# Two matmuls with the same weights made one of 512 columns, and a down unit moved between the products of the up projection

## The chip, the cores and the metric

The kernel runs on one core of a Trainium2 chip. Its engines work side by side, each through its own queue in a fixed order: TensorE (PE in the profile, its weight loads PEld), VectorE (DVE), ScalarE (ACT), GpSimd (POOL) and SyncE (SP), the last two issuing transfers here. The metric is the device time of one execution in microseconds (us), as a median of several runs.

## The reference

One layer of an encoder on 512 positions with 2048 channels, in float32: a normalisation, an input projection, two token mixers (a convolution module and a neighbourhood attention), an output projection, and then the gated MLP that matters here:

```python
xn = rms_norm(x, ffn_norm_g[l])
up = jnp.einsum("bsd,df->bsf", xn, w_up[l])          # 2048 -> 2 * 5632
up = depthwise_conv(up, ffn_dw_w[l], ffn_dw_b[l])    # 3 taps over positions
gate, val = jnp.split(up, 2, axis=-1)
x = x + jnp.einsum("bsf,fd->bsd", jax.nn.silu(gate) * val, w_down[l])
```

A last normalisation follows.

## The kernel before, in words

**Two parts for each number.** To keep float32 accuracy, each operand of a product is held as a high part (rounded to the matmul's format, fp32r) and a low part (the rest). A product is then three matmuls, in mm3 (L116 to L121): high weights by high data (L119), high weights by low data (L120), low weights by high data (L121). Weights come from memory as units of 128x1024 (raw, L103), and parts (L105) splits each: ScalarE copies it to whi (L108), VectorE subtracts to get wlo (L109). There are three buffers each of whi and wlo. weights() makes units two ahead of their use, in the order of the list plan. So a unit's split can only start when the unit three places before it has been used up.

**The up projection** computes its product by a scheme with seven products in place of eight. The 2048 channels are taken as two halves (even and odd blocks of 128) and the positions as two halves of H = 256. For one block f of 128 gate and 128 value columns, factors (L524) makes the seven weight factors out of four loaded units, with four sums on VectorE (L531 to L537; the running sum is ws). The seven data factors are made once, before the up projection, by halves (L486): each is one tile xc of 128x512 whose first 256 columns are the high part and whose last 256 the low part. up(f) (L562) runs the seven products, each of eight steps of 128 channels with three matmuls of 256 columns into the first half of a PSUM bank (pu), and adds them up on the way: two copies on ScalarE (L576, L577) and seven adds of 128x256 on VectorE (L578 to L585). Products one to six use three PSUM banks in turn, so product four takes the bank of product one; product seven has a bank of its own. hidden(f) (L597) then multiplies by the norm's factor (L599, L600, the latter with -1), convolves gate and value (conv3, L588: one scaled copy on ScalarE and two taps on VectorE each), applies silu (L602) and multiplies (L603).

**The down projection** follows in chunks of CH = 4 blocks. in_two (L606) splits the four results of a chunk into hh and hl. The next chunk's blocks carry its 16 output tiles as eight down units: a unit is one weight unit, two output tiles, four steps and three wide matmuls each, so 24 matmuls of 512 columns (pd). Each output tile is copied by ScalarE (pdc, L621) and added to the sum in memory by an accumulating transfer from POOL (L622).

**Order.** The main loop (L625) goes through 11 chunks of 4 blocks, 44 in all. Within a block come seven products, then the convolution, and behind it two down units of the chunk before. The first chunk has none; in the last chunk the first block has none, the next two have two each, and the four others come behind the last block. The last chunk's own down projection stands at the end, in half positions. A scheduler lays out each engine's queue at build time from this program order and from its own estimate of durations; at run time each engine keeps that order. Almost all small tiles share 79 buffers of 2 KB for each partition (t2).

Of the kernel before, what the change touches and what calls it, by code (L numbers as in the profile page):

```python
# [30 lines left out]
KD = D // P  # L31
NC_ = CONV // P
NP_ = HEADS // 2
NF = FF // P
U = 8
# [5 lines left out]
H = S // 2  # L41
CH = 4
NCH = NF // CH
# [11 lines left out]
POFF = {}  # L55
# [8 lines left out]
def layer(ctx: ExitStack, tc: tile.TileContext, xT, w_in, w_out, w_up, w_down, par, tab, out):  # L64
    nc = tc.nc
    consts = ctx.enter_context(tc.tile_pool(name="consts", bufs=1))
# [4 lines left out]
    psm = ctx.enter_context(tc.tile_pool(name="psm", bufs=3, space=bass.MemoryType.PSUM))  # L71
# [10 lines left out]
    def t2(name, dt=F32):  # L82
        return tp.tile([P, S], dt, tag="t2k", name=name)
# [28 lines left out]
    def unit(src, n):  # L112

        return parts(raw_unit(src, n)[0], n)[:2]

    def mm3(ps, w, wk, mh, ml, start, stop):  # L116
        hi, lo = w[:2]
        a = slice(wk * P, (wk + 1) * P)
        nc.tensor.matmul(ps, hi[:, a], mh, start=start, stop=False)  # L119
        nc.tensor.matmul(ps, hi[:, a], ml, start=False, stop=False)  # L120
        return nc.tensor.matmul(ps, lo[:, a], mh, start=False, stop=stop)  # L121
# [83 lines left out]
    for k in range(KD):  # L205
        x1.append(t2("x"))
        last = pin(nc.sync.dma_start(x1[k], xT[k]))
# [223 lines left out]
    p, n = -1, 0  # L431
# [54 lines left out]
    def halves(src, c):  # L486

        t = t2("xc", F32R)
        nc.scalar.activation(t[:, :H], src, AF.Copy)
        nc.vector.tensor_sub(t[:, H:], src, t[:, :H].bitcast(F32))  # L490
        comb[c].append((t[:, :H], t[:, H:]))

    def after(d, ps):

# [23 lines left out]

    rstd2 = []

    def stats2():
        rstd2.append((yield from rsqrt_steps(acc2, D, "rstd2")))

    def factors(f):  # L524

        def make(c):
            if c == 0:
                a[:] = [raw_unit(w_up[f, q], U * P)[0] for q in range(4)] + [t4([P, U * P], "ws")]
            a11, a21, a22, a12, s_ = a
            if c == 1:  # L530
                add(s_, a21, a22)  # L531
            elif c == 2:
                add(s_, s_, a11)
            elif c == 4:
                add(a21, a21, a11)
            elif c == 5:
                add(s_, s_, a12)  # L537
            return parts((a11, s_, s_, a12, a21, s_, a22)[c], U * P)[:2]

        a = []  # L540
        return [lambda c=c: make(c) for c in range(7)]

    add = nc.vector.tensor_add

    def down_units(c, i):
# [12 lines left out]

    out_half(mb, after)
    steps.append(stats2())  # L560

    def up(f):  # L562

        def product(c):
            w = weights()
            ps = (psa.tile([P, S], F32, tag="po", name="pu") if c == 6 else
                  psm.tile([P, S], F32, tag="mm", name="pu"))[:, :H]
            for k in range(U):
                m = mm3(ps, w, k, *comb[c][k], k == 0, k == U - 1)
            tick(m)  # L570
            return ps

        uu, vv = t2("u"), t2("v")
        u, t, u2 = uu[:, :H], uu[:, H:], vv[:, :H]
        g, v = t2("g"), t2("vl")
        nc.scalar.activation(u, product(0), AF.Copy)  # L576
# [8 lines left out]
        add(v[:, :H], u2, product(6))  # L585
        return g, v

    def conv3(a, n):  # L588
        y = t2("uy")
        o = POFF["fww"] + 3 * n  # L590
        nc.scalar.activation(y, a, AF.Identity, scale=prm[:, o + 1:o + 2], bias=pc("fwb", n))
        nc.vector.scalar_tensor_tensor(y[:, 1:], a[:, :S - 1], prm[:, o:o + 1], y[:, 1:], op0=ALU.mult, op1=ALU.add)
        nc.vector.scalar_tensor_tensor(y[:, :S - 1], a[:, 1:], prm[:, o + 2:o + 3], y[:, :S - 1],
                                       op0=ALU.mult, op1=ALU.add)
        return y

    def hidden(f):  # L597
        g, v = up(f)
        nc.vector.tensor_mul(g, g, rstd2[0])  # L599
        nc.vector.scalar_tensor_tensor(v, v, -1.0, rstd2[0], op0=ALU.mult, op1=ALU.mult)  # L600
        g, v = conv3(g, f), conv3(v, NF + f)
        nc.scalar.activation(g, g, AF.Silu)  # L602
        nc.vector.tensor_mul(g, g, v)  # L603
        return g

    def in_two(g):  # L606
        h, l = t2("hh", F32R), t2("hl", F32R)
        nc.scalar.activation(h, g, AF.Copy)
        nc.vector.tensor_sub(l, g, h.bitcast(F32))
        return h, l  # L610

    def down(hs, ds):

        for d0 in ds:
            w = weights()
            for d in range(d0, d0 + U // CH):
                ps = psa.tile([P, S], F32, tag="tr", name="pd", bufs=2)
                for k in range(CH):
                    mm3(ps, w, (d - d0) * CH + k, *hs[k], k == 0, k == CH - 1)
                t = t2("pdc")  # L620
                nc.scalar.activation(t, ps, AF.Copy)  # L621
# [12 lines left out]
    n = CH  # L634
    x2 = []
# [95 lines left out]
```

## Time and profile before

| what | us |
|---|---|
| median of 3 runs | 2103.06 |
| lowest and highest | 2101.43, 2103.21 |
| the profiled execution | 2101.72 |
| its span, first to last instruction | 2099.9 |
| mean granted TensorE clock | 0.996 of full speed |

How to read the profile: a group row names source line, engine, operation, and output from inputs by tile names, then the shape; after the bar stand the group's busy time with the mean duration of one, and then the idle time of the engine just before such instructions, with what ended it. In the timeline a row starts with the start time and the duration, in us from the start of the span; "[1.90 <-PE pd]" means that the engine was idle for 1.90 us before and that this ended it. Matmuls, and most operations of VectorE and ScalarE, overlap with the one behind them, so a cost is read from start to start, not from the duration.

Where the time lies, by TensorE's starts: 8.5 to 502 us the input projection with the mixers beside it, to 699 the output projection, 699 to 2034 the up and down projections, to 2084 the last chunk's down projection.

### The profile page before, as it was taken

How to read it: one execution, taken by the hardware profiler on the slowest of the kernel's cores; microseconds unless marked ns; L12 is line 12 of the kernel's file. 1: busy time of each engine (PE TensorE's matmuls, PEld its weight loads, DVE VectorE, ACT ScalarE, POOL GpSimd, SP SyncE). 2: the span in 40 equal slices, each digit the busy share in tenths (PEclk: the TensorE clock that was granted, in tenths of full speed). 3: DMA queues.
4: the chain of work that ended last, by engine and by line, in shares of the span. 5: the costliest groups of instructions: out<-in, count | busy, mean ns of one | idle time of the engine just before them, and what ended most of it. 6: DMA issues, size and time to landing. Idle time of an engine off the chain costs nothing.

```text
span 2099.9 us, 32453 instructions
## 1 busy us (share of the span) xinstructions
PE 2061.7 (98%) x13024; PEld 1851.1 (88%) x13024; DVE 1585.8 (76%) x2180; ACT 985.3 (47%) x1428; POOL 140.0 (7%) x166
## 2 busy tenths in 40 slices
PE   8999999999999999999999999999999999999997
PEld 6888888877778899999999999999999999999987
DVE  7985796686568898777777778777777777878756
ACT  6234424447436544444444444454454444545452
POOL 0000000000000000110110110110111011010110
PEclk9999999999999999999999999999999999999998
DMA  6333223335324244555555565665565555554672
GB/s 237 101 111 110 81 81 110 101 101 200 116 96 140 71 121 124 138 130 143 130 139 143 122 146 135 132 140 136 137 140 127 144 131 138 144 121 123 147 193 81
DMA packets 95911, 270.90 MB, mean 129 GB/s; under 512 B 10640, under 2 KB 14736, under 8 KB 95760
## 3 DMA queue, kind: packets, MB, share of 16 engines
q1 hardware_dynamic: 72720, 226.88, 33.7%
q0 software_dynamic: 23040, 41.95, 14.7%
q8 instruction: 102, 1.67, 0.3%
q14 instruction: 49, 0.40, 0.1%
HBM read 218.46 MB, written 50.33 MB: 128 GB/s over the span
## 4 chain that ended last, share of the span: by engine, by line
PE 94%; DVE 4%; DMA 1%; ACT 1%; issue 0%; SPq 0%; DVEq 0%; ACTq 0%
PE pu L121 13%; PE pu L119 13%; PE pu L120 13%; PE pd L119 8%; PE pd L120 8%; PE pd L121 8%; PE pj L119 7%; PE pj L121 7%; PE pj L120 7%; PE po L119 2%; PE po L120 2%; PE po L121 2%; DVE wlo L109 1%; PE sc L365 1%; PE po L408 1%; PE trp L395 1%
## 5 line engine op out<-in xcount | busy, mean ns | idle before, releaser
L121 PE MATMUL pu<-xc,wlo 128*128 128x256 f32 x2464 | 697.8, 283 | 2.1 <-DVE wlo L109 2.1
L108 ACT ACTIVATE whi<-raw 128x1024 fp32r<-128x1024 f32 x368 | 389.4, 1059 | 660.0 <-PE pu L120 299.3
L119 PE MATMUL pu<-xc,whi 128*128 128x256 f32 x2464 | 698.3, 283 | 0.8 <-ACT whi L108 0.7
L120 PE MATMUL pu<-xc,whi 128*128 128x256 f32 x2464 | 698.0, 283 | 0.0
L109 DVE TENSOR_TENSOR wlo<-raw,whi 128x1024 fp32r<-128x1024 f32 x368 | 449.1, 1222 | 171.6 <-ACT whi L108 143.9
L121 PEld LDWEIGHTS pu<-xc,wlo 128*128 128x128 f32 x2464 | 473.3, 192 | 3.2 <-DVE wlo L109 3.2
L119 PEld LDWEIGHTS pu<-xc,whi 128*128 128x128 f32 x2464 | 473.5, 192 | 2.9 <-ACT whi L108 1.2
L120 PEld LDWEIGHTS pu<-xc,whi 128*128 128x128 f32 x2464 | 473.6, 192 | 1.9 <-issue 0.2
L109 DVE TENSOR_TENSOR wlo<-ws,whi 128x1024 fp32r<-128x1024 f32 x132 | 161.5, 1223 | 160.2 <-ACT whi L108 159.7
L622 POOL DMA_DIRECT2D x2d<-pdc x160 | 139.3, 873 | 1896.0 <-ACT pdc L621 1893.4
L119 PE MATMUL pj<-xh,whi 128*128 128x512 f32 x640 | 254.1, 398 | 8.5 <-ACT whi L108 8.5
L121 PE MATMUL pj<-xh,wlo 128*128 128x512 f32 x640 | 250.3, 391 | 1.7 <-DVE wlo L109 1.7
L119 PE MATMUL pd<-hh,whi 128*128 128x512 f32 x640 | 249.6, 390 | 1.9 <-ACT pdc L621 1.9
L120 PE MATMUL pj<-xl,whi 128*128 128x512 f32 x640 | 250.3, 391 | 0.0
L108 ACT ACTIVATE whi<-ws 128x1024 fp32r<-128x1024 f32 x132 | 139.9, 1060 | 233.7 <-PE pd L120 142.4
L120 PE MATMUL pd<-hl,whi 128*128 128x512 f32 x640 | 249.5, 390 | 0.0
L121 PE MATMUL pd<-hh,wlo 128*128 128x512 f32 x640 | 249.0, 389 | 0.0
L279 DVE SCALAR_TENSOR_TENSOR y<-ch,prm,y 128x504 f32<-128x504 f32 (+14 forms) x240 | 170.2, 741 | 3.2
L119 PEld LDWEIGHTS pj<-xh,whi 128*128 128x128 f32 x640 | 120.7, 189 | 37.0 <-ACT whi L108 10.5
L121 PEld LDWEIGHTS pj<-xh,wlo 128*128 128x128 f32 x640 | 120.5, 188 | 29.1 <-DVE wlo L109 3.6
L119 PEld LDWEIGHTS pd<-hh,whi 128*128 128x128 f32 x640 | 120.3, 188 | 26.3 <-ACT pdc L621 2.3
L121 PEld LDWEIGHTS pd<-hh,wlo 128*128 128x128 f32 x640 | 120.1, 188 | 25.3
(141 smaller groups left out, 2403.4 us busy)
## 6 DMA issues: line engine op xcount, KB each, us to landing
raw<-in_w_up SPq DMA_DIRECT2D x176, 512.0 KB, 4.1
raw<-in_w_down SPq DMA_DIRECT2D x88, 512.0 KB, 3.7
raw<-in_w_in SPq DMA_DIRECT2D x80, 512.0 KB, 3.6
x2d<-pdc POOLq DMA_DIRECT2D x160, 256.0 KB, 4.2
raw<-in_w_out SPq DMA_DIRECT2D x32, 512.0 KB, 3.5
x<-in_xT SPq DMA_DIRECT2D x32, 256.0 KB, 6.0
tab<-in_tab SPq DMA_DIRECT2D x32, 256.0 KB, 4.0
x2d<-x SPq DMA_DIRECT2D x16, 256.0 KB, 2.0
```

What stands on the lines that cost most here:

```text
L108: i = nc.scalar.activation(hi[:, :n], raw[:, :n], AF.Copy)
L109: j = nc.vector.tensor_sub(lo[:, :n], raw[:, :n], hi[:, :n].bitcast(F32))
L119: nc.tensor.matmul(ps, hi[:, a], mh, start=start, stop=False)
L120: nc.tensor.matmul(ps, hi[:, a], ml, start=False, stop=False)
L121: return nc.tensor.matmul(ps, lo[:, a], mh, start=False, stop=stop)
L279: nc.vector.scalar_tensor_tensor(y[:, a:b], h[:, a + j - PAD:b + j - PAD], prm[:, o + j:o + j + 1], y[:, a:b], op0=ALU.mult, op1=ALU.add)
L365: m = nc.tensor.matmul(both[:, j, i, :], q[hp, b * P:(b + 1) * P], grid(k, KC0[b], KW)[hp], start=True, stop=True)
L395: m = nc.tensor.transpose(ps[:, 2 * i + ch, :], s[:, i, ch * P:(ch + 1) * P], ident)
L408: m = nc.tensor.matmul(grid(po, b * BLK, BLK)[hp], vt[b // 2][:, 2 * (b % 2) + ch, hp], pts[j][:, 2 * i + ch, :], start=(ch == 0), stop=(c ...
L622: nc.gpsimd.dma_start(xd[d], t, accum_op=ALU.add)
```

## The change

In each of the eight steps of a product of the up projection, the two matmuls with whi (by the high and by the low data) become one of 512 columns over the whole tile xc, so the low data's product comes out in the second half of the PSUM bank; the matmul with wlo adds to that second half. A product therefore leaves a main half and a leftover half that must be added: ScalarE copies the leftover half to a small tile (pl), and VectorE adds. In place of seven adds of 128x256 there are ten of 128x256 and two of 128x512: one makes both value sums by reading its input twice, one adds the two gate leftovers. The minus sign of L600 moves into a copy of the value taps (fwn), made once. The down units are no longer two behind the block: one stands behind the fourth product and one behind the seventh; both are issued inside up, through the callback between. In the last block of the last chunk none runs inside, and in_two stands ahead of the four left over.

```diff
-        comb[c].append((t[:, :H], t[:, H:]))
+        comb[c].append(t)
...
+    fwn = consts.tile([P, 3 * NF], F32, name="fwn")
+    nc.vector.tensor_scalar(fwn, prm[:, POFF["fww"] + 3 * NF:POFF["fww"] + 6 * NF], -1.0, None, op0=ALU.mult)
...
-    def down_units(c, i):
+    def down_units(c, i, at):
-        at = [0, 4, 8, 12, 16] if c < NCH - 1 else [0, 0, 4, 8, 16]
-        return range(at[i], at[i + 1], U // CH) if c else ()
+        n = U // CH
+        if not c:
+            return ()
+        if c < NCH - 1:
+            return {3: (4 * i,), 6: (4 * i + n,)}.get(at, ())
+        return {(1, 3): (0,), (1, 6): (2,), (2, 3): (4,), (2, 6): (6,), (3, 6): range(8, KD, n)}.get((i, at), ())
...
-            plan.extend(factors(c * CH + i))
-            for d0 in down_units(c, i):
-                plan.append(lambda c=c, d0=d0: unit(down_weights((c - 1) * CH, d0), U * P))
+            for at, make in enumerate(factors(c * CH + i)):
+                plan.append(make)
+                for d0 in down_units(c, i, at):
+                    plan.append(lambda c=c, d0=d0: unit(down_weights((c - 1) * CH, d0), U * P))
...
-    def up(f):
+    def up(f, between):
         def product(c):
             w = weights()
             ps = (psa.tile([P, S], F32, tag="po", name="pu") if c == 6 else
-                  psm.tile([P, S], F32, tag="mm", name="pu"))[:, :H]
+                  psm.tile([P, S], F32, tag="mm", name="pu"))
             for k in range(U):
-                m = mm3(ps, w, k, *comb[c][k], k == 0, k == U - 1)
-            tick(m)
-            return ps
+                hi, lo = (w[i][:, k * P:(k + 1) * P] for i in range(2))
+                m = comb[c][k]
+                wide = lambda: nc.tensor.matmul(ps, hi, m, start=k == 0, stop=k == U - 1)
+                low = lambda: nc.tensor.matmul(ps[:, H:], lo, m[:, :H], start=False, stop=False)
+                if k < U - 1:
+                    wide()
+                    i = low()
+                else:
+                    low()
+                    i = wide()
+            tick(i)
+            between(c)
+            return ps[:, :H], ps[:, H:]
+        def low_part(ps):
+            t = t2("pl")[:, :H]
+            nc.scalar.activation(t, ps, AF.Copy)
+            return t
...
-        nc.scalar.activation(u, product(0), AF.Copy)
-        nc.scalar.activation(t, product(1), AF.Copy)
-        add(u2, u, product(2))
+        m, l = product(0)
+        add(u, m, low_part(l))
+        m, l = product(1)
+        add(t, m, low_part(l))
+        m, l = product(2)
+        l = low_part(l)
+        add(u2, u, m)
+        add(u2, u2, l)
         add(t, t, u2)
-        add(g[:, :H], u, product(3))
-        ps = product(4)
-        add(u2, u2, ps)
-        add(v[:, H:], t, ps)
-        add(g[:, H:], t, product(5))
-        add(v[:, :H], u2, product(6))
+        low = t2("pl")
+        m, l = product(3)
+        nc.scalar.activation(low[:, :H], l, AF.Copy)
+        add(g[:, :H], u, m)
+        m, l = product(4)
+        add(u, m, low_part(l))
+        add(v.rearrange("p (i t) -> p i t", i=2), uu, u.unsqueeze(1).broadcast_to([P, 2, H]))
+        m, l = product(5)
+        nc.scalar.activation(low[:, H:], l, AF.Copy)
+        add(g[:, H:], t, m)
+        add(g, g, low)
+        m, l = product(6)
+        l = low_part(l)
+        add(v[:, :H], v[:, :H], m)
+        add(v[:, :H], v[:, :H], l)
         return g, v
...
-        nc.vector.scalar_tensor_tensor(v, v, -1.0, rstd2[0], op0=ALU.mult, op1=ALU.mult)
+        nc.vector.tensor_mul(v, v, rstd2[0])
...
-            hs.append(hidden(c * CH + i))
-            if c == NCH - 1 and i == CH - 1:
-                hs = [in_two(h) for h in hs]
-            down(pend, down_units(c, i))
-        pend = hs if c == NCH - 1 else [in_two(h) for h in hs]
+            last = c == NCH - 1 and i == CH - 1
+            hs.append(hidden(c * CH + i, lambda at: None if last else down(pend, down_units(c, i, at))))
+        hs = [in_two(h) for h in hs]
+        if last:
+            down(pend, down_units(c, i, 6))
+        pend = hs
```

More of the change, by code (lines that the diff above doesn't have):

```diff
@@ L566, in product @@
             ps = (psa.tile([P, S], F32, tag="po", name="pu") if c == 6 else
-                  psm.tile([P, S], F32, tag="mm", name="pu"))[:, :H]
+                  psm.tile([P, S], F32, tag="mm", name="pu"))
             for k in range(U):
-                m = mm3(ps, w, k, *comb[c][k], k == 0, k == U - 1)
-            tick(m)
-            return ps
[L573 to L576, printed above, removed]
@@ new lines, in product @@
+                low = lambda: nc.tensor.matmul(ps[:, H:], lo, m[:, :H], start=False, stop=False)
[12 more added lines that the diff above has]
+            return t
+        u = t2("u")[:, :H]
@@ new lines, in up @@
+        uu = t2("uu").rearrange("p (i t) -> p i t", i=2)
+        u2, t = uu[:, 0], uu[:, 1]
+        g = t2("g")
+        v = t2("vl")
+        m, l = product(0)
[6 more added lines that the diff above has]
+        add(u2, u2, l)
+        add(t, t, u2)
+        low = t2("pl")
+        m, l = product(3)
+        nc.scalar.activation(low[:, :H], l, AF.Copy)
+        add(g[:, :H], u, m)
@@ L590, in conv3, with hidden @@
         o = POFF["fww"] + 3 * n
-        nc.scalar.activation(y, a, AF.Identity, scale=prm[:, o + 1:o + 2], bias=pc("fwb", n))
-        nc.vector.scalar_tensor_tensor(y[:, 1:], a[:, :S - 1], prm[:, o:o + 1], y[:, 1:], op0=ALU.mult, op1=ALU.add)
-        nc.vector.scalar_tensor_tensor(y[:, :S - 1], a[:, 1:], prm[:, o + 2:o + 3], y[:, :S - 1],
+        w, o = (prm, o) if n < NF else (fwn, o - POFF["fww"] - 3 * NF)
+        nc.scalar.activation(y, a, AF.Identity, scale=w[:, o + 1:o + 2], bias=pc("fwb", n))
+        nc.vector.scalar_tensor_tensor(y[:, 1:], a[:, :S - 1], w[:, o:o + 1], y[:, 1:], op0=ALU.mult, op1=ALU.add)
+        nc.vector.scalar_tensor_tensor(y[:, :S - 1], a[:, 1:], w[:, o + 2:o + 3], y[:, :S - 1],
                                        op0=ALU.mult, op1=ALU.add)
         return y
-    def hidden(f):
-        g, v = up(f)
+    def hidden(f, between):
+        g, v = up(f, between)
         nc.vector.tensor_mul(g, g, rstd2[0])
-        nc.vector.scalar_tensor_tensor(v, v, -1.0, rstd2[0], op0=ALU.mult, op1=ALU.mult)
+        nc.vector.tensor_mul(v, v, rstd2[0])
         g, v = conv3(g, f), conv3(v, NF + f)
```

## The prediction

> **What bounds the kernel now.** I read the page from the top: span and busy time, then the chain of work that ended last, then the groups of instructions.
>
> ```profile
> span 2099.9 us, 32453 instructions
> PE 2061.7 (98%) x13024; PEld 1851.1 (88%) x13024; DVE 1585.8 (76%) x2180; ACT 985.3 (47%) x1428; POOL 140.0 (7%) x166
> ...
> PE 94%; DVE 4%; DMA 1%; ACT 1%; issue 0%; SPq 0%; DVEq 0%; ACTq 0%
> PE pu L121 13%; PE pu L119 13%; PE pu L120 13%; PE pd L119 8%; PE pd L120 8%; PE pd L121 8%; PE pj L119 7%; PE pj L121 7%; PE pj L120 7%; PE po L119 2%; PE po L120 2%; PE po L121 2%; DVE wlo L109 1%; PE sc L365 1%; PE po L408 1%; PE trp L395 1%
> ...
> L121 PE MATMUL pu<-xc,wlo 128*128 128x256 f32 x2464 | 697.8, 283 | 2.1 <-DVE wlo L109 2.1
> ```
>
> TensorE is 94% of the chain, the up projection's three matmul lines alone 39%. The group row says the same from the other side: before 2464 matmuls on L121 TensorE was idle for 2.1 us in all. So today what counts is the spacing of the matmuls, not a wait. Their 283 ns is no spacing, because they overlap; that is read from start to start, in the timeline of TensorE across one pair of down units:
>
> ```profile
> 1299.76 0.28 PE L121 MATMUL pu<-xc,wlo 128*128 128x256 f32 x1
> ...
> 1306.96 0.28 PE L121 MATMUL pu<-xc,wlo 128*128 128x256 f32 x1
> 1307.08 0.40 PE L119 MATMUL pd<-hh,whi 128*128 128x512 f32 x1
> 1307.32 0.40 PE L120 MATMUL pd<-hl,whi 128*128 128x512 f32 x1
> ...
> 1317.76 0.39 PE L121 MATMUL pd<-hh,wlo 128*128 128x512 f32 x1
> 1317.99 0.28 PE L119 MATMUL pu<-xc,whi 128*128 128x256 f32 x1
> 1318.10 0.28 PE L120 MATMUL pu<-xc,whi 128*128 128x256 f32 x1
> ```
>
> From 1299.76 to 1306.96 lie 60 narrow (256-column) starts, 0.120 us each; from 1307.32 to 1317.76 lie 46 wide (512-column) ones, 0.227 us each. Two narrow ones cost 0.240, one wide 0.227: about 13 ns per matmul do not depend on its width. That is what the merge can save.
>
> The second view is the windows, for how full VectorE is (the columns are length, then PE, PEld, DVE, ACT, POOL busy, clock, DMA share, GB/s):
>
> ```profile
> 752.00:772.00 20.00, 19.73 (x165) 19.53 (x164) 18.97 (x25) 9.23 (x12) 0.00 (x0) 1.00 0.37 106
> 1300.00:1600.00 300.00, 300.00 (x2074) 281.06 (x2073) 224.03 (x270) 143.56 (x182) 34.49 (x40) 1.00 0.59 137
> ```
>
> In the first chunk, where blocks have no down units, VectorE is busy 95%: there it sets the pace already. Later it is at 75% and TensorE at 100%. ScalarE is at half in both. I call one call of hidden a block; there are 44, four to a chunk.
>
> **The change, part by part. 1. Matmuls removed.** Each of 44 x 7 x 8 = 2464 steps has three narrow matmuls (0.360 us) now and one wide plus one narrow afterwards. No row shows them alternating. By the two spacings the pair is 0.227 + 0.120 = 0.347. At the change of width the rows above show 0.24 for the first wide after a narrow and 0.11 for the first narrow after a wide: 0.350. I take 0.348, between these, so 12 ns saved per step: **-29.6 us** (ends -32.0 and -24.6). A product goes from 2.88 to 2.784 us, a regular block from 31.06 to 30.4.
>
> **2. Work added.** Per block ScalarE gets five more copies of 128x256 out of PSUM; at half busy, and with its time spent in waits for TensorE, it hides them. VectorE's adds go from seven of 128x256 to ten, plus two of 128x512. What that costs is again read from start to start:
>
> ```profile
> 747.37 0.42 DVE L585 TENSOR_TENSOR vl<-v,pu 128x256 f32<-128x256 f32 x1
> ...
> 766.23 1.22 DVE L109 TENSOR_TENSOR wlo<-ws,whi 128x1024 fp32r<-128x1024 f32 x1
> 767.37 0.75 DVE L592 SCALAR_TENSOR_TENSOR uy<-g,prm,uy 128x511 f32<-128x511 f32 x1
> 768.04 0.42 DVE L585 TENSOR_TENSOR vl<-v,pu 128x256 f32<-128x256 f32 x1
> 768.38 0.75 DVE L593 SCALAR_TENSOR_TENSOR uy<-g,prm,uy 128x511 f32<-128x511 f32 x1
> 769.05 0.68 DVE L600 SCALAR_TENSOR_TENSOR vl<-vl,rstd 128x512 f32<-128x512 f32 x1
> 769.65 1.22 DVE L533 TENSOR_TENSOR ws<-ws,raw 128x1024 f32<-128x1024 f32 x1
> 770.78 0.74 DVE L592 SCALAR_TENSOR_TENSOR uy<-vl,prm,uy 128x511 f32<-128x511 f32 x1
> ...
> 788.73 0.42 DVE L585 TENSOR_TENSOR vl<-v,pu 128x256 f32<-128x256 f32 x1
> ...
> 810.33 0.42 DVE L585 TENSOR_TENSOR vl<-v,pu 128x256 f32<-128x256 f32 x1
> ```
>
> A weight split takes 1.14, a convolution tap 0.67, a 128x256 add 0.34, a 128x512 one 0.60, a weight sum 1.13. So the block's VectorE work grows by 3 x 0.34 + 2 x 0.60 = 2.2 us. L585 is the last read of a block, so its rows also give the period: 20.67 and 20.69 for blocks 2 and 3 against 168 x 0.120 = 20.16 of matmuls.
>
> In the first chunk nothing covers the 2.2 us. By these intervals a block without down units has 7 x 1.14 + 4 x 1.13 + 7 x 0.34 + 4 x 0.67 + 3 x 0.60 = 19.4 us now (1.3 of 20.7 idle) and 21.6 afterwards. In the changed order VectorE's read of the sixth product still waits for TensorE, which I put at 0.5 us: 22.1 instead of 20.7. Against the 20.0 that part 1 credits that is 2.1 each for blocks 1 to 3: **+6.3 us**. Block 4 adds the chunk's four hl and meets the first down unit; from L585 of block 3 to the end of block 4's down units it is 21.6 + 10.9 now. Afterwards I count 28.4 to the last product, as product four waits for a bank read that stands behind the hl, and 5.4 for the second down unit: 33.8, against 31.8 credited, **+2.0 us**.
>
> **3. Regular blocks** (29, with two down units each and no chunk boundary). Take the start of a block's first product as zero. Today's rows at the end of a down unit, which ends at 1317.99:
>
> ```profile
> 1317.96 1.06 ACT L108 ACTIVATE whi<-ws 128x1024 fp32r<-128x1024 f32 x1 [1.90 <-PE pd L120]
> 1318.93 0.58 ACT L621 ACTIVATE pdc<-pd 128x512 f32<-128x512 f32 x1
> 1319.06 1.23 DVE L109 TENSOR_TENSOR wlo<-ws,whi 128x1024 fp32r<-128x1024 f32 x1 [2.95 <-ACT whi L108]
> ```
>
> The third product's weights take the down unit's buffer, so VectorE starts its split at 1.07. In the changed order follow: an add (2.21), a tap that waits for ScalarE, then add, tap, multiply, the split for product four, a tap, and at 6.6 the read that frees the first product's PSUM, done at 7.05. Product four, which takes that bank, starts at 8.35: 1.3 us to spare. The split for the down unit ends at 9.8 and is needed at 11.6. VectorE's busy 75% of 31.06 are 23.2 us; with 2.2 more, 25.4 fit into 30.4, and the moved down unit spreads them. **0 us**, and the price if this cover goes is in rival C.
>
> The wait of that tap: ScalarE does the down unit's copy, the sixth product's leftover copy and the convolution's scale first:
>
> ```profile
> 790.45 0.82 ACT L591 ACTIVATE uy<-vl,prm 128x512 f32<-128x512 f32 x1
> 791.17 0.61 ACT L608 ACTIVATE hh<-uy 128x512 fp32r<-128x512 f32 x1
> ...
> 796.09 0.36 ACT L576 ACTIVATE u<-pu 128x256 f32<-128x256 f32 x1
> ```
>
> ScalarE's rows overlap by 0.1 (790.45 + 0.82 against 791.17), so 0.94 + 0.48 + 0.27 + 0.82 = 2.51, and the tap starts at 2.56.
>
> **4. Chunk boundaries.** Before, the first down unit of a chunk stood behind all seven products, some 20 us after in_two began. Now it stands behind the third or fourth, and in the built order of the changed kernel it comes after product three, while VectorE has the four hl subtractions ahead of that unit's weight split. From 2.56: tap 0.67, add 0.34, tap 0.67, multiply 0.60, split 1.14, tap 0.67, hl 0.60, tap 0.67, hl 0.60, multiply 0.60, hl 0.60 makes 9.72; the split ends 1.22 later at 10.94. TensorE arrives at 3 x 2.784 = 8.35, can do four wide matmuls with the high part, and needs the low part at 9.26; with the weight load it goes on at about 11.1: a stall of 1.8 us. Product four behind it waits for the bank read at 11.9, which the next five matmuls cover. Eight boundaries (blocks 8 to 36): **+14.4 us** (ends 0 and 8 x 3 = 24). At block 40 there is no down unit to put first, so product four waits for that bank, from 8.35 to 11.95: **+3.6 us**. Behind block 43 the 21.7 us of down units cover in_two, as now.
>
> **5. The rest at nothing.** The negated taps are made once, 0.2 us beside the first loads; tensor_mul for L600 has the same size. SP's loads of the down weights are asked for two units ahead as before, and by the changed order their buffers come free 10 us or more before the use. POOL has four accumulating transfers per block in two pairs instead of one group, at 7% busy. The new small tiles reuse buffers that such a transfer reads, but by the changed order those lie half a block back, against 4 us of a transfer.
>
> **Sum:** -29.6 + 6.3 + 2.0 + 14.4 + 3.6 = -3.3 us. The profiled execution took 2101.72 us, 1.8 over its span; it comes to 2098.4. The median of the runs shown, 2103.06, is 1.3 above it: **2099.8 us**.
>
> **Rivals.** **B: no stall at boundaries**, because VectorE gets ahead (a shorter wait for the tap, hl earlier). For it: VectorE idles 2.95 us just before zero in the row at 1319.06. Against it: that idle time is a wait for the buffer, which stays. Without the 14.4: 2103.06 - 17.7 = 2085.4.
>
> **C, slower: VectorE also late in regular blocks.** Its place is the read that frees the first product's bank before product four; it decides from a delay of 1.3 us. With 1.7 us of delay, 29 blocks lose 0.4 and eight boundaries 1.7: 25.2 us more, 2125. For it: twelve instructions behind each other with durations from another stage, and new reads of PSUM. Against it: none of them waits long by my count.
>
> **D: the fixed 13 ns is not saved**, because each change of width costs what the first wide one showed (0.24 instead of 0.227) and the narrow one gives nothing back. Then the stalls stand alone: 2103.06 + 26.3 = 2129. Against it is the 0.11 at 1318.10. [...]
>
> That the change does not do what it says is out: in its built order each product has eight wide and eight narrow matmuls.
>
> **How the numbers follow.** Chances: forecast 0.45 (own range 2094 to 2108: both ends of part 1, and half a us at each boundary), B 0.22, C 0.20, D 0.13. The range goes from 2082 (B with 0.347) to 2130 (D); outside lie about a fifth of B, a third of C and part of D, some 0.15. About 0.2%, 4.2 us, is what a measurement of this kernel can tell from no change: faster is below 2098.9, slower above 2107.3. Faster: B and two fifths of the forecast, 0.41; slower: C, D and a sliver, 0.35; within: 0.24.
>
> **What would show it.** Right: pu steps at 0.348 in the timeline; regular blocks of 30.4 from last read to last read; first-chunk blocks of 22; TensorE waiting for wlo about 1.8 us eight times, and about 3.6 once at block 40 for a read of PSUM. Wrong: steps at 0.36 (D), regular blocks over 30.6 with waits for VectorE (C), or boundaries as long as their neighbours (B).

## The result, and the profile after

The changed kernel is slower: 2115.64 us against 2102.62 for the kernel before, medians of four runs each, a ratio of 1.0062 (95% interval 1.0045 to 1.008). The forecast was 2099.8.

The page of the changed kernel's profiled execution (2115.82 us), and the two groups of the up projection's matmuls:

```profile
span 2114.0 us, 27919 instructions
PE 2054.8 (97%) x10560; PEld 1723.3 (82%) x10560; DVE 1664.5 (79%) x2401; ACT 1037.7 (49%) x1648; POOL 140.1 (7%) x166
...
L580 PE MATMUL pu<-xc,whi 128*128 128x512 f32 x2464 | 865.4, 399 | 8.6 <-DVE u L604 5.8
L581 PE MATMUL pu<-xc,wlo 128*128 128x256 f32 x2464 | 644.0, 282 | 2.4 <-DVE wlo L109 2.4
```

The merge did what it says: 2464 wide and 2464 narrow matmuls stand where 7392 narrow ones were. Yet TensorE is still busy 97%, and the idle time in front of a few matmuls is new. The waits of TensorE (total, times, longest, in us) name them:

```profile
PE pd L121 <- DVE wlo L109: 11.6, 8, 1.4
...
PE pu L580 <- DVE u L604: 5.8, 2, 3.4
...
PE pd L119 <- ACT pdc L664: 3.6, 1, 3.6
```

Eight waits of a down unit for wlo are the eight chunk boundaries; the 3.4 for a read of PSUM (L604) is block 40; the wait for pdc is in the last block, and was 1.9 before. Two rows of VectorE's timeline lie a block apart; here are the last reads (L627) of blocks 18, 19, 20 and 21:

```profile
1265.93 0.42 DVE L627 TENSOR_TENSOR vl<-vl,pl 128x256 f32<-128x256 f32 x1
...
1296.56 0.42 DVE L627 TENSOR_TENSOR vl<-vl,pl 128x256 f32<-128x256 f32 x1
...
1328.96 0.42 DVE L627 TENSOR_TENSOR vl<-vl,pl 128x256 f32<-128x256 f32 x1
...
1359.60 0.42 DVE L627 TENSOR_TENSOR vl<-vl,pl 128x256 f32<-128x256 f32 x1
```

A regular block takes 30.63 us, where 30.4 was forecast and 31.06 stood before. The block behind a boundary (20 is the first of a chunk) takes 32.40, 1.77 more than its neighbours. VectorE's queue at that place shows why:

```profile
1299.96 0.69 DVE L652 TENSOR_TENSOR hl<-uy,hh 128x512 fp32r<-128x512 f32 x1
...
1301.22 0.69 DVE L652 TENSOR_TENSOR hl<-uy,hh 128x512 fp32r<-128x512 f32 x1
...
1302.42 0.68 DVE L652 TENSOR_TENSOR hl<-uy,hh 128x512 fp32r<-128x512 f32 x1
1303.03 1.22 DVE L109 TENSOR_TENSOR wlo<-raw,whi 128x1024 fp32r<-128x1024 f32 x1
1304.16 0.68 DVE L652 TENSOR_TENSOR hl<-uy,hh 128x512 fp32r<-128x512 f32 x1
```

Three of the four hl stand ahead of the split (L109) of the down unit's weights, the fourth behind it, and VectorE has no gap. TensorE's own timeline shows both, the spacing and the stall:

```profile
1299.29 0.40 PE L580 MATMUL pu<-xc,whi 128*128 128x512 f32 x1
1299.52 0.28 PE L581 MATMUL pu<-xc,wlo 128*128 128x256 f32 x1
...
1301.06 0.40 PE L580 MATMUL pu<-xc,whi 128*128 128x512 f32 x1
...
1302.46 0.40 PE L120 MATMUL pd<-hl,whi 128*128 128x512 f32 x1
1304.30 0.51 PE L121 MATMUL pd<-hh,wlo 128*128 128x512 f32 x1 [1.45 <-DVE wlo L109]
```

From 1299.29 to 1301.06 lie five steps of a wide and a narrow matmul, 0.354 us each. Over all 1036 pairs from 1240 to 1900 us the wide one takes 0.2352 from start to start and the narrow one 0.1173: 0.3525, not 0.348.

The third cause is in no list of waits. The windows show it. Columns are length, busy time of PE, PEld, DVE, ACT and POOL, then the granted clock. First around the gap at 591 us, where TensorE waits 3.6 us for oa in the output projection, which the change doesn't touch; then around block 40's stall:

```profile
590.87:594.29 3.42, 0.63 (x3) 0.19 (x1) 3.39 (x6) 1.67 (x2) 0.00 (x0) 1.00 0.42 156
594.29:597.70 3.41, 2.62 (x6) 2.15 (x7) 3.38 (x7) 0.00 (x0) 0.00 (x0) 0.50 0.49 154
597.70:601.11 3.41, 3.41 (x9) 2.64 (x8) 0.36 (x1) 0.00 (x0) 0.00 (x0) 0.50 0.00 0
...
1922.07:1925.48 3.41, 1.35 (x8) 0.92 (x6) 3.41 (x6) 2.47 (x6) 0.00 (x0) 1.00 0.00 0
1925.48:1928.90 3.42, 2.08 (x7) 1.81 (x8) 3.39 (x8) 0.40 (x2) 0.00 (x0) 0.50 0.49 153
1928.90:1932.31 3.41, 3.41 (x12) 2.93 (x12) 1.59 (x2) 0.66 (x1) 0.00 (x0) 0.50 0.68 185
```

Behind the slices of 3.41 us in which TensorE was busy for only 0.63 and 1.35 us, the next two ran at half the clock, 0.50. The kernel before has the same gap at 591, but its profiled execution shared it out over two slices, busy 1.68 and 1.56 us each, and the clock stayed up:

```profile
590.03:593.45 3.42, 1.68 (x8) 1.06 (x6) 3.40 (x5) 1.67 (x2) 0.00 (x0) 1.00 0.29 93
593.45:596.86 3.41, 1.56 (x7) 1.33 (x8) 3.41 (x6) 0.00 (x0) 0.00 (x0) 1.00 0.66 215
```

In the changed kernel's profiled execution four places have such slices that the kernel before's has not: 594 (6.83 us), 806 (3.41), 1925 (6.83) and 2031 us (3.41).

Where the time went, in the two profiled executions, by the starts of each block's first matmul on TensorE. The last column is the sum of the prediction's own terms for that stretch:

| stretch | before, us | after, us | difference | forecast |
|---|---|---|---|---|
| up to the first product | 698.78 | 701.36 | +2.6 | 0 |
| blocks 0 to 3 | 89.75 | 91.29 | +1.5 | +3.6 |
| block 4 | 32.51 | 35.84 | +3.3 | +1.3 |
| blocks 5 to 39, eight boundaries among them | 1087.10 | 1086.32 | -0.8 | -9.1 |
| block 40 | 20.15 | 25.85 | +5.7 | +2.9 |
| blocks 41 to 43, to the last matmul of the up projection | 82.16 | 80.76 | -1.4 | -2.0 |
| behind it | 89.51 | 92.60 | +3.1 | 0 |
| sum | 2099.9 | 2114.0 | +14.0 | -3.3 |

### The profile page after: what moved, and what is told of

Its sections match the earlier page's. It is cut to its first block, busy times and chain, and to the rows that moved or that the text cites. A ratio compares the mean times of both kernels' runs of the same rounds, so it can differ in the third digit from the quotient of the medians.

```text
span 2114.0 us, 27919 instructions
## 1 busy us (share of the span) xinstructions
PE 2054.8 (97%) x10560; PEld 1723.3 (82%) x10560; DVE 1664.5 (79%) x2401; ACT 1037.7 (49%) x1648; POOL 140.1 (7%) x166
## 4 chain that ended last, share of the span: by engine, by line
issue 50%; PE 36%; POOL 6%; DVE 4%; DMA 2%; ACT 1%; SPq 0%; POOLq 0%; DVEq 0%; ACTq 0%
PE pj L119 7%; PE pj L121 6%; PE pj L120 6%; POOL x2d L665 6%; PE pu L580 2%; PE po L119 2%; PE po L120 2%; PE po L121 2%; PE pu L581 1%; PE pd L119 1%; PE pd L121 1%; PE pd L120 1%; DVE wlo L109 1%; PE sc L365 1%; PE po L408 1%
## 5 line engine op out<-in xcount | busy, mean ns | idle before, releaser
L580 PE MATMUL pu<-xc,whi 128*128 128x512 f32 x2464 | 865.4, 399 | 8.6 <-DVE u L604 5.8
L581 PE MATMUL pu<-xc,wlo 128*128 128x256 f32 x2464 | 644.0, 282 | 2.4 <-DVE wlo L109 2.4
L109 DVE TENSOR_TENSOR wlo<-raw,whi 128x1024 fp32r<-128x1024 f32 x368 | 448.9, 1221 | 142.7 <-ACT whi L108 113.5
L580 PEld LDWEIGHTS pu<-xc,whi 128*128 128x128 f32 x2464 | 450.9, 189 | 99.6 <-ACT whi L108 4.3
L581 PEld LDWEIGHTS pu<-xc,wlo 128*128 128x128 f32 x2464 | 467.2, 190 | 32.5 <-DVE wlo L109 5.0
L109 DVE TENSOR_TENSOR wlo<-ws,whi 128x1024 fp32r<-128x1024 f32 x132 | 161.5, 1223 | 127.9 <-ACT whi L108 127.9
L120 PEld LDWEIGHTS pd<-hl,whi 128*128 128x128 f32 x640 | 120.6, 188 | 25.4
L120 PEld LDWEIGHTS pj<-xl,whi 128*128 128x128 f32 x640 | 120.8, 189 | 24.6 <-issue 0.7
```

What stands on the lines that cost most here:

```text
L109: j = nc.vector.tensor_sub(lo[:, :n], raw[:, :n], hi[:, :n].bitcast(F32))
L580: wide = lambda: nc.tensor.matmul(ps, hi, m, start=k == 0, stop=k == U - 1)
L581: low = lambda: nc.tensor.matmul(ps[:, H:], lo, m[:, :H], start=False, stop=False)
```

## The experiments

Theory after this reading: a step saves 7.5 ns instead of 12; the moved units add the forecast boundary stalls; and idle stretches cost more than their length, by the clock behind them. Rivals: VectorE is late in every block; the boundary stall comes from the plan of the weights; the half speed belongs to something else.

| kernel | median, us | ratio to the kernel before (95% interval) |
|---|---|---|
| the changed kernel | 2115.64 | 1.0062 (1.0045 to 1.008) |
| e1, merge alone | 2099.90 | 0.9984 (0.9974 to 0.9993) |
| e2, placement alone | 2110.84 | 1.0035 (1.0022 to 1.0048) |
| e3, grouped | 2103.43 | 0.9999 (0.999 to 1.0008) |
| e4, halves spread | 2091.77 | 0.9947 (0.993 to 0.9963) |
| e5, gap filled | 2113.79 | 1.0049 (1.0034 to 1.0064) |
| e6, before, shifted | 2104.08 | 1.0005 (0.9996 to 1.0014) |
| e7, spread and grouped | 2083.93 | 0.9907 (0.989 to 0.9923) |
| e8, combined | 2079.90 | 0.9890 (0.9875 to 0.9904) |
| e10, before, gap filled | 2101.72 | 0.9992 (0.9983 to 1.0001) |

e9 (2109.29 us) and e11 (2107.05 us) are single executions, read from their traces. The kernel before, run beside each group, had medians of 2102.62 to 2103.38.

**e1, the merge alone.** In the changed kernel the plan and the loop of the kernel before:

```diff
-            hs.append(hidden(c * CH + i, lambda at: None if last else down(pend, down_units(c, i, at))))
+            hs.append(hidden(c * CH + i))
+            if c == NCH - 1 and i == CH - 1:
+                hs = [in_two(h) for h in hs]
+            down(pend, down_units(c, i))
```

> The merge alone: the changed kernel with the down units behind the block again, where the kernel before has them. Theory (the changed kernel's trace: a step of a wide and a low matmul takes 0.353 us, not the 0.348 that was forecast; the placed units bring eight boundary stalls of 1.8 us; idle stretches of over 2 us inside one 3.41 us slice of a fixed grid halve the granted clock in the next slices): the boundary stalls and most of the 3.8 us at block 40 go, with them the half-speed slices at 806 and 1925 us (1.7 and 3.4 us), regular blocks stay at 30.63 us: 2092 to 2098 us. Rival (the units have to stand inside the block because VectorE is late in every block with the merged matmul): about 1 us of wait in each of 40 blocks, 2130 us or more.

2099.90 us, 15.7 under the changed kernel and 2 over the theory's stretch. Regular blocks stay at 30.63, the boundary blocks fall to 30.94, block 40 to 20.0: most of the stall belongs to the placement (0.31 us at each boundary stays). VectorE isn't late in every block, so that rival is out. What missed: those 0.31 us, 2.5 at eight boundaries, and block 4, where TensorE waits 3.6 us for a read of PSUM (2.3 in the changed kernel) and a half-speed slice follows, as no unit stands in front.

**e2, the placement alone.** The kernel before, with its narrow matmuls, and the changed kernel's plan, callback and loop:

```diff
             tick(m)
+            between(c)
             return ps
...
-            hs.append(hidden(c * CH + i))
+            hs.append(hidden(c * CH + i, lambda at: None if last else down(pend, down_units(c, i, at))))
```

> The placement alone: the kernel before with its three narrow matmuls, the down units behind the fourth and the seventh product as in the changed kernel. Theory (the four hl of a chunk stand on VectorE ahead of the wlo that the first unit needs, whatever the matmuls are; VectorE has about 1.4 us less to do in a block here): a stall of 0.5 to 1.8 us at each of eight boundaries, 2106 to 2117 us, blocks otherwise at 31.06 us. Rival (placement is harmless, the stall is made by the merge's additional adds): 2102 to 2104 us, and no wait of a down unit for wlo.

2110.84 us: the placement by itself costs 7.5 us. The boundary block takes 31.73 against 31.08, a stall of 0.65. But the wait that shows isn't the one the theory named. The waits of TensorE in this kernel:

```profile
PE pu L119 <- ACT u L582: 4.2, 9, 1.3
```

Nine times (eight boundaries and block 40) it waits for ScalarE's copy of a product. In ScalarE's queue that copy (L582) stands behind the chunk's last hh and a weight copy, and the last hh waits for VectorE's last multiply (L609) among the hl:

```profile
1297.47 0.63 ACT L614 ACTIVATE hh<-uy 128x512 fp32r<-128x512 f32 x1 [0.45 <-DVE uy L609]
1298.17 1.06 ACT L108 ACTIVATE whi<-raw 128x1024 fp32r<-128x1024 f32 x1
1299.13 0.36 ACT L582 ACTIVATE u<-pu 128x256 f32<-128x256 f32 x1
...
1299.55 0.39 PE L119 MATMUL pu<-xc,whi 128*128 128x256 f32 x1 [0.37 <-ACT u L582]
```

The same bunch of work, another end of it. One by one, the edits make -3.5 and +7.5, together +4.0; both at once make +13.0. In the profiled executions 5.9 us of what they make beyond their sum lie in blocks 5 to 39 and 4.3 in block 40; other stretches give a part back. At a boundary it is VectorE's queue: from the split of the third product's weights to that of the down unit's it is 7.38 us long in e2 and 8.61 in the changed kernel (1294.42 to 1303.03), where the last product's two adds and a multiply stand in between.

**e3, grouped.** Seven wide matmuls, the eight low ones, the last wide one:

```diff
-                if k < U - 1:
-                    wide()
-                    i = low()
-                else:
-                    low()
-                    i = wide()
+            for k in range(U - 1):
+                wide(k)
+            for k in range(U):
+                nc.tensor.matmul(ps[:, H:], w[1][:, k * P:(k + 1) * P], comb[c][k][:, :H], start=False, stop=False)
+            i = wide(U - 1)
```

> The changed kernel with the order inside a product changed: seven wide matmuls, then the eight low ones, then the last wide one, so that wide follows wide and low follows low. Theory (the missing 5 to 6 ns of a step come from the alternation of 512 and 256 columns): the step falls from 0.353 to 0.347 us, 56 steps in each of 40 blocks, about 13 us less: 2100 to 2104 us, regular blocks at 30.3 us. Rival (a wide matmul of the up projection takes 0.233 us whatever stands ahead of it): no change, 2114 to 2117 us.

2103.43 us, in the theory's stretch, but not for the theory's reason alone: regular blocks fall to 30.43, a step to 0.3491 and not to 0.347. That is 0.20 us in 40 blocks, 8 us; the rest came from blocks 0 to 4 and 40 and from the stretch up to the first product, where this execution also had fewer half-speed slices (mean clock 0.994 against 0.992). TensorE's timeline, where eight equal matmuls are one row:

```profile
1398.19 2.00 PE L578 MATMUL pu<-xc,whi 128*128 128x512 f32 x8
1400.03 1.11 PE L583 MATMUL pu<-xc,wlo 128*128 128x256 f32 x8
1400.99 2.00 PE L578 MATMUL pu<-xc,whi 128*128 128x512 f32 x8
```

Eight wide ones take 1.84 us, 0.230 each, not 0.227; eight narrow ones 0.96, 0.120. By position, the first five wide ones behind narrow ones take 233, 236, 228, 232 and 231 ns, and from the sixth on it is 226.7. The kernel before has the same five numbers where a down unit follows a product. So in these two traces the first five wide matmuls behind narrow ones took 2 to 9 ns more than the later ones; the first two narrow ones behind a wide run gave 8 ns back (113 and 119 instead of 120).

**e9, in twos.** The same, in short runs:

```diff
+            for k in range(0, U - 2, 2):
+                wide(k)
+                wide(k + 1)
+                low(k)
+                low(k + 1)
+            wide(U - 2)
+            low(U - 2)
+            low(U - 1)
+            i = wide(U - 1)
```

> The changed kernel with wide and low matmuls in twos: runs of three, two, two and one wide per product with two low ones between. Theory (the traces of the kernel before and of e3 show that the first five wide ones behind narrow ones take 233, 236, 228, 232 and 231 ns and only then 226.7): short runs get almost nothing, 697 + 2 x 469 + 234 for the wide and about 944 for the low ones, 2.813 us for a product and 30.57 us for a regular block. Rival (each change of width has a fixed price, half as many changes give half of what no change would): 30.40 us or less, under the 30.43 of e3.

Regular blocks take 30.56 us, forecast 30.57, not 30.40: short runs gain 0.07 us where the grouping of e3 gained 0.20. What inside TensorE makes the five is open; no run tells it.

**e4, halves spread.** hh and hl of the chunk behind the first products of the next:

```diff
+            def between(at):
+                if c and i == 0 and at < 3:
+                    pend.extend(in_two(h) for h in raw[at:at + 1 + at // 2])
+                if not last:
+                    down(pend, down_units(c, i, at))
...
-        hs = [in_two(h) for h in hs]
+        if c < NCH - 1:
+            raw, pend = hs, []
```

> The changed kernel with the four hh and hl of a chunk made behind products one, two and three of the next chunk's first block, not all four behind the chunk's last block. Theory (the boundary stall is VectorE's four hl in a row ahead of the first unit's wlo): the eight stalls of 1.8 us go (14.2 us), block 40 falls from 24.7 to 22 or 23 us and the half-speed slices at 806 and 1925 us (1.7 and 3.4 us) go: 2094 to 2100 us. Rival (the stall comes from the lead with which the plan makes the unit's weights): the stalls stay, 2113 to 2117 us.

2091.77 us, 23.9 under the changed kernel, 0.5% under the kernel before and 2.2 better than the theory's stretch. The waits of TensorE, longest first:

```profile
PE pj L119 <- ACT whi L108: 8.0, 1, 8.0
PE st L185 <- DVE dg L182: 4.3, 2, 2.2
PE po L119 <- DVE oa L475: 3.6, 1, 3.6
PE pd L119 <- ACT pdc L664: 3.5, 1, 3.5
```

The waits of the down units for wlo are gone with the plan as it was, so the plan's lead wasn't the cause; blocks behind a boundary take 30.6 to 30.7. Block 40 falls from 25.85 to 20.62 and the half-speed slices at 806 and 1925 are gone (mean clock 0.995 against 0.992): there is no idle time left that brings them.

**e5, the gap filled.** In the output projection ahead of the block that waits, in the changed kernel:

```diff
+            if m is ma and d == 13:
+                fill = psa.tile([P, S], F32, tag="tr", name="fill", bufs=2)
+                for _ in range(14):
+                    nc.tensor.matmul(fill, m[0][0][:, :P], m[0][0], start=True, stop=True)
```

> The changed kernel with 14 more matmuls of 512 columns, whose result nothing reads, in the gap of 3.6 us in which TensorE waits for oa at 591 us (14 x 0.2265 = 3.2 us). Theory (an idle stretch that takes more than about 2 us of one 3.41 us slice of a fixed grid makes the granted clock 0.5 for the next one or two slices): work is added on the bounding engine and the kernel gets faster, by half of the 6.83 us that run at half speed: 2111 to 2114 us, no half-speed slice between 590 and 602 us. Rival (the half speed there is no matter of idleness, or costs nothing because that stage waits for VectorE): 2115 to 2117 us.

2113.79 us: 1.85 under the changed kernel's median, 2.7 by the two ratios; their intervals overlap, so the time alone doesn't decide it. The clock does. A window over the whole place:

```profile
590.00:602.00 12.00, 11.58 (x52) 9.31 (x51) 9.19 (x14) 2.42 (x4) 0.00 (x0) 1.00 0.27 89
```

The clock is 1.00 throughout, where 6.83 us were at 0.50, and 3.2 us of added work did not make the kernel slower.

**e6, the kernel before, shifted.** In project, ahead of the last one's own matmuls:

```diff
+        if n == 2 * NC_ + 2 * NP_ + NP_ - 1:
+            for _ in range(6):
+                nc.tensor.matmul(ps, xs[0][0][:, :P], xs[0][0], start=True, stop=True)
```

> The kernel before with 6 more matmuls of 512 columns, whose result nothing reads, ahead of the last projection, so that all behind it comes 1.36 us later against the grid of slices. Theory (its gap of 3.6 us at 591 us was shared by two slices, 1.7 and 1.9 us idle, and so left the clock alone; 1.4 us later nearly all of it lies in one slice): a half-speed slice behind the gap, 3.41 or 6.83 us long, so 1.4 us of work cost 3.1 to 4.8 us: 2106 to 2108.5 us. Rival (the half speed belongs to the changed kernel's instructions, not to where a gap falls on the grid): 1.4 us more, 2104 to 2105 us, clock as before.

The slice came, the time did not: 2104.08 us, what the rival had.

```profile
592.11:595.52 3.41, 0.38 (x2) 0.00 (x0) 3.39 (x5) 1.67 (x2) 0.00 (x0) 1.00 0.44 156
595.52:598.93 3.41, 2.86 (x7) 2.31 (x8) 3.38 (x6) 0.00 (x0) 0.00 (x0) 0.50 0.45 154
```

One part of the theory falls here: the grid is not fixed to the program. Its first mark lies at 13.2 us of the span in the kernel before, at 14.0 in the changed one, at 11.8 here, and between 11.5 and 15.2 in all 13 traces, more than a whole slice apart. Then most executions of the kernel before should have the slice behind 591 too, its median should contain it, and its profiled one was lucky.

**e10, the kernel before with the gap filled** tests just that, with the edit of e5.

> The kernel before with the 14 matmuls that nothing reads in its gap at 591 us, as in e5. Theory (the grid of slices lies otherwise against the program in each execution, so that the gap halves the clock in most executions of the kernel before as well, and its profiled execution was a lucky one): 1 to 3 us faster than the kernel before, 2100 to 2102 us, with no half-speed slice between 590 and 602 us. Rival (the kernel before has none there): no change, 2102.5 to 2103.5 us.

2101.72 us against 2103.22, as expected, though the interval just reaches 1. The clock tells it better: the mean is 0.9963 over 11 runs against 0.9953 over 15 of the kernel before beside them, 2 us of clock, about one slice, and the window has no slice at half speed:

```profile
590.00:602.00 12.00, 11.58 (x52) 9.27 (x51) 9.15 (x14) 2.38 (x4) 0.00 (x0) 1.00 0.26 89
```

This profiled execution is the slowest of the eleven (2103.77): it has a half-speed slice at 2019 us, behind the wait of 1.9 us for pdc that the kernel before's passed with the clock up. Both clocks are given to three places, so the theory is supported here rather than settled.

**e11, fewer adds.** Three adds of leftovers are left to the later chunks:

```diff
-        add(u2, u2, l)
+        if f >= CH:
+            add(u2, u2, l)
...
-        add(g, g, low)
+        if f >= CH:
+            add(g, g, low)
...
-        add(v[:, :H], v[:, :H], l)
+        if f >= CH:
+            add(v[:, :H], v[:, :H], l)
```

> The changed kernel without three adds of leftovers in each block of the first chunk (two of 128x256, one of 128x512, 1.28 us by the intervals of the kernel before); it leaves these sums out of the first four blocks' values, so it tells only of time. Theory (VectorE's adds set the pace of blocks 1 to 3): the three blocks fall from 21.0, 21.7 and 22.2 us, 64.9 in all, to about 61 to 62, near TensorE's 19.8 each. Rival (their pace is set by how soon weight buffers come free, through ScalarE and TensorE): 64 us or more.

Blocks 1 to 3 take 61.2 us instead of 64.9. The window of these blocks in the changed kernel (behind the length, PE, PEld and DVE):

```profile
727.00:792.00 65.00, 60.93 (x338) 50.95 (x337) 63.32 (x89) 35.47 (x52) 0.00 (x0) 1.00 0.31 97
```

The same 65 us in e11:

```profile
727.00:792.00 65.00, 63.63 (x359) 54.60 (x358) 63.94 (x86) 38.04 (x56) 0.00 (x0) 1.00 0.34 106
```

VectorE is full in both (97 and 98%), and with less to do for a block TensorE gets more matmuls through: VectorE sets the pace of the first chunk.

**e7 and e8, what the runs point to.** e7 puts e3's and e4's edits together. e8 adds e5's, and in the last block every second down unit takes the two PSUM banks that the attention's scores leave free:

```diff
+            both = psa.tile([P, 2, S], F32, tag="sc", name="pd") if spare and d0 // 2 % 2 == 0 else None
...
-                ps = psa.tile([P, S], F32, tag="tr", name="pd", bufs=2)
+                ps = both[:, d - d0] if both is not None else psa.tile([P, S], F32, tag="tr", name="pd", bufs=2)
```

> The two single edits that gained, together: halves spread over the next block's products, and wide and low matmuls grouped. Theory (stalls and spacing are independent terms): the stalls of e4 stay away and each of 40 blocks falls by 0.20 us, as grouping alone did: 2091.8 less 8 to 12 us, 2080 to 2084 us. Rival (grouping makes TensorE want wlo later and whi sooner, so that without the boundary stalls it waits for ScalarE or VectorE in the blocks): 2086 us or more.

> As e7, and the gap at 591 us filled with the 14 matmuls that nothing reads, and in the last block every second down unit in the PSUM banks that the attention's scores leave free, so that TensorE needn't wait 3.5 us there for an eviction. Theory: the wait of 3.5 us goes, with it the half-speed slice behind it (1.7 us), and the slice behind the filled gap (1.7 us): 6 to 7 us under e7, 2074 to 2078 us. Rival (the eviction that is waited for stands behind the last block's tail on ScalarE, so the wait only comes two tiles later): 2 us under e7.

e7: 2083.93 us, the two gains add up (7.8 under e4). e8: 2079.90, 1.1% under the kernel before; its gain of 4.0 is less than the 6 to 7 expected. The wait for pdc only shrank, and which of the two edits gained how much no run separates:

```profile
PE pd L119 <- ACT pdc L665: 2.5, 2, 1.8
...
PE po L119 <- DVE oa L479: 0.4, 1, 0.4
```

## Why the prediction was wrong

**Part 1, the matmuls removed, is the term that was mis-sized.** It took 12 ns a step; 7.5 are saved (0.360 to 0.3525), 0.43 us a block instead of 0.67. Over blocks 5 to 39 that makes 35 x 0.245 = 8.6 us, about what the forecast missed there (8.3), and over 2464 steps 18.5 us saved where 29.6 were put down. The ends were wrong too: 0.347 and 0.350 both fall short of 0.3525. The prediction read the price of a change of width off a single change, in rows rounded to 10 ns, to settle a question of 5 ns. More readings of that kind would not have helped: over the 22 such changes between 1240 and 1900 us of the same trace, the first wide matmul behind a narrow one takes 233 ns and the first narrow one behind a wide one 113, 0.3466 us together. That trace has long runs of one width only, and what alternating costs (0.2352 and 0.1173) stands in none of its rows. Rival D was partly right: 5.8 of the fixed 13 ns are not saved. But most of it is, 7.5 ns.

**Part 2, VectorE's load in the first chunk, held.** Forecast 22.1 for blocks 1 to 3, measured 21.0, 21.7 and 22.2; e11 shows that it is VectorE's adds. Some 2 us too much was charged there.

**Part 3, regular blocks without a stall, held**: the changed kernel, e1 and e4 alike have all 27 of them between blocks 5 and 39 at 30.63. Rival C is out.

**Part 4, the boundaries, held in place, cause and size**: 1.8 forecast and 1.77 measured, eight times, and e4 takes it away by moving hh and hl alone; rival B is out. Counted from the start of block 20's first product (1293.31), the split that TensorE waits for runs from 9.72 to 10.94 us, the two times that the prediction had added up. Its sentence has four hl ahead of that split, its sum three, and three it is. At block 40 the forecast 3.6 us came as a gap of 3.8 from start to start. What it left out is behind the gap, in the two half-speed slices:

```profile
1927.60 0.63 PE L580 MATMUL pu<-xc,whi 128*128 128x512 f32 x1
1928.03 0.41 PE L581 MATMUL pu<-xc,wlo 128*128 128x256 f32 x1
1928.24 0.63 PE L580 MATMUL pu<-xc,whi 128*128 128x512 f32 x1
```

A step takes 0.64 us there, not 0.3525 (and not twice that, 0.705). TensorE worked in 5.5 us of the two slices, so they cost about 2.5 us, an estimate (5.5 us less 5.5 x 0.3525 / 0.64).

**Part 5, the rest at nothing, failed** in two ways. The wait for pdc in the last block grew from 1.9 to 3.6 us. The merge brings it: it is 3.5 in e1 and 1.9 in e2. ScalarE copies pdc behind the last hh, which waits for VectorE's last multiply, and from VectorE's read of the last product to that multiply it takes 6.7 us now (L626 at 2022.28, L646 at 2028.93), 5.3 before (L585 at 2010.76, L603 at 2016.03). The prediction had said that the 21.7 us of units cover in_two, and never looked at the eviction behind it in ScalarE's queue. And nothing had been set down for the clock. In the profiled executions the half-speed slices explain most of the +2.6 up to the first product, about 1.5 at block 4, 2.5 at block 40 and 1.6 at the end. In the average execution it is less, since the slice at 591 seems to be common to both kernels: the mean clock is 0.9923 over the four runs of the changed kernel and 0.9954 over 48 of the kernel before, which makes about 6.6 us. That number is from clocks given to three places, so it may be off by one; and it is rather an upper end, since TensorE is idle in a tenth of the added half-speed slices and loses a little less than half in the rest (0.64 us a step against 0.3525). Some 5 to 7 us is as close as these runs come.

So of the 16.3 us between the forecast change (-3.3) and the measured one (+13.0), the step accounts for about 9.8 (40 blocks by 0.245), the clock for 5 to 7 and the eviction for 1.7, less the 2 that were charged too much in the first chunk. By these sums the change would have come out 2 to 4 us faster without the first two; without only one of them it would still not have been faster.

## What to carry to other kernels

Read the price of a matmul shape from many pairs in the order in which they will stand; where no row has that order, run it before relying on it (here other orders gave 0.347 us and the new one 0.3525). Prefer long runs of one width (a step took 0.3491 us in e3, 0.3525 where the widths alternate). Work that a later stage needs in a bunch (here four hh and hl) belongs between the products ahead of its use, above all when a change moves that use forward: spreading it turned a loss of 0.6% into a gain of 0.5%. A stall of TensorE of about 2 us or more cost its length in these traces and, where enough of it fell into one slice of 3.41 us, an estimated 1.5 to 3 us of lost speed on top (the half-speed slices of the changed kernel, by 0.64 us a step against 0.3525).

## What the runs showed of the hardware

**The clock goes by slices.** In all 13 traces the granted clock changes only on a grid of 3.413 us, and only between 1.00 and 0.50; in the changed kernel's trace it stays at 1.00 for 580.27 us, 170 such slices, from the first mark to the fall at 594.29. With TensorE's idle time worked out for each full-speed slice behind the first 30 us and ahead of the last normalisation, none with up to 1.85 us idle (the slice at 593.45 us of the kernel before) was followed by a half-speed slice, and all 35 with 1.92 us or more were (1.92 at 710.34 us of the changed kernel; the other four there have 2.07, 2.34, 2.79 and 2.93, the one of the kernel before, at 709.50 us, 2.02). In the last normalisation, where the clock falls once more in each trace, 12 of the 13 slices ahead of that have 2.13 us idle or more (2.44 in the kernel before, 2.22 in the changed one), but the one of e2 has 1.48, so the bound is not a law. So a gap of 3.6 us passed unseen where the grid cut it in two (1.73 and 1.85 us idle in the kernel before), and one of 2.3 us cost an estimated 1.5 more (the slice behind the one at 802.5 us of the changed kernel, 3.41 us at 0.64 us a step instead of 0.3525). The grid's first mark differs from trace to trace (13.2, 14.0 and 11.8 us in the kernel before, the changed one and e6), so whether such a gap was paid for depended on how the grid happened to lie.

**The first five wide matmuls behind narrow ones were slower**: 233, 236, 228, 232, 231 and then 226.7 ns from start to start, in the kernel before and in e3 alike, and 235 for each wide one where the widths alternate (the changed kernel). The narrow ones behind a wide run took 113, 119 and then 120.0, and 117 where the widths alternate.

**At half the clock these matmuls ran at a little more than half the speed.** Wide ones in a row took 0.427 us (2031.46 to 2032.74 us of the changed kernel, three of them), 0.227 at full clock, and a pair of a wide and a narrow one 0.64 (1927.60 to 1928.24 us), 0.3525 at full clock, which leaves 0.213 for the narrow one. That is in proportion to the columns: the 13 ns that did not depend on the width at full clock (2 x 0.120 less 0.227) don't show at half.
